# Prompt-attention masks moved from TensorE into VectorE's maximum, and the compression gather split into halves of eight tokens with two buffers

## The chip, the cores and the metric

The kernel runs on one NeuronCore of a Trainium2 chip as a single launch. The metric is the device time of one execution in microseconds (us). The core's engines run side by side: TensorE (PE; its weight loads are listed as PEld), VectorE (DVE), ScalarE (ACT), GpSimd (POOL) and SyncE (SP, which here only issues DMAs). Each works through its own instructions in a fixed order and waits for the others at semaphores.

## The reference, cut to what matters

One step of a decoder layer for two groups of requests: a prompt of 1024 tokens, and 8 samples with 8 new tokens each and 2048 cached ones. The layer is a half feed-forward, a mixer (attention beside a state-space branch), and a second half feed-forward. Attention has 8 query heads over 2 key/value heads of 64, and three branches: compressed blocks, selected blocks and a window of 512. With 16 blocks of 64 covering all 1024 prompt tokens, a prompt query's selected branch is plain causal attention. The parts that the change touches:

```
# masked softmax of each branch; the window branch adds dist < 512
def masked_softmax(s, mask):
    s = jnp.where(mask, s.astype(jnp.float32), NEG)
    e = jnp.where(mask, jnp.exp(s - jnp.max(s, axis=-1, keepdims=True)), 0.0)
    return e / jnp.maximum(jnp.sum(e, axis=-1, keepdims=True), 1e-30)
...
# compression of the cached rows: windows of 32 tokens, stride 16, through a two-layer MLP
    ch = rows[:, :nc * CMP_STRIDE].reshape(b, nc, CMP_STRIDE, KV_HEADS, HEAD_DIM)
    blk = jnp.concatenate([ch[:, :-1], ch[:, 1:]], axis=2) + pe[None, None, :, None, :]
    blk = blk.transpose(0, 1, 3, 2, 4).reshape(b, nc - 1, KV_HEADS, CMP_BLOCK * HEAD_DIM)
    return jax.nn.silu(blk @ w1) @ w2
```

## The kernel before, in words

The program is written in layer order, but the order of instructions on each engine is set at build time by a scheduler that follows data dependences, buffer reuse and modelled durations. Pools with a fixed number of buffers (`bufs`) say when a tile can be written again. A table `KN` picks the engine of each copy or scaling, and the order of the query tiles.

The stage concerned is the loop over eight tiles of 128 prompt queries (L1751), in the order 2, 7, 6, 5, 4, 3, 1, 0. Two things are written into this loop.

**Prompt attention.** For each tile there are two key/value groups of four heads, and two branches: branch 0 sees all keys up to the tile, branch 1 (window) the last five key tiles at most. Per head and branch the keys are cut into one part of up to 512 keys or two parts. Each part is one bank of PSUM, from three buffers (`s2`) that the compressed branch's scores share. Two fp32r matmuls (L1808, L1810) form the scores with the positional bias. The mask is added on TensorE: a bf16 matmul of the identity with a 128x128 mask of zeros and very large negative numbers adds it into the last 128 columns of the part (`mdiag`, causal) or the first 128 (`medge`, window edge), L1813. VectorE takes the negated maximum (L1818, or L1821 per part and L1822 over the two). ScalarE computes the exponential from PSUM into `pb` in SBUF and its sum (L1824). `pb` is scaled by the gate over the sum on POOL, ACT or DVE (L275 to L279), transposed on TensorE (L1846), copied out of PSUM to `pt` (L267), and multiplied with the values (L1855). `pb` has five buffers per branch.

**Compression of the samples.** `compress_sample` runs for the eight samples, at places that `KN["cs"]` gives: three before the first query tile, then 0, 2, 1, 1, 0, 1, 0. One indirect DMA on POOL's queue (L1689) gathers a sample's rows into `chk` (128 chunks of 16 tokens, 16 KB each, 2 MB in all), with a single buffer. Eight steps (keys, then values, four steps each) follow: ACT and POOL copy four tokens into `chp`, TensorE transposes them to `cT` (L1712), ACT casts the upper part `th`, DVE forms the remainder `tl` (L1717), and twelve matmuls accumulate into `cA` (L1733 to L1735). At the end of keys and of values follow a SiLU and a small product `c` (L1740, L1743). The copies of step `jj` read tokens 4jj to 4jj+3 of the buffer, once for keys and once for values.

**What comes next.** The sample attention uses the memory that this stage's pools give back when they close. Its first transfers therefore wait for the last matmul of compression, which reads the last tile of these pools: on SP's queue two window loads of `schk` (L2052), `big` (2.3 MB, L1951), four loads of `xT` and the loads of the output projection's weights `raw` (L1900); on POOL's queue the gathers of `schk` (L2048, 512 KB each). The output projection (`wout`, L250 to L252) and the sample attention's transposes (`kT_ps`, L2064) are the first work on TensorE after the stage.

Of the kernel before, what the change touches and what calls it, by code (L numbers as in the profile page):

```python
# [10 lines left out]
F32 = mybir.dt.float32  # L11
# [7 lines left out]
P = 128  # L19
# [22 lines left out]
def f32(ap):  # L42
    return ap.bitcast(F32)
# [37 lines left out]
def hybrid_step(ctx: ExitStack, tc: tile.TileContext, *aps):  # L81
# [1499 lines left out]
    AC = Ds.enter_context(pool("attc"))  # L1581
    mdiag = AC.tile([P, P], BF16, name="mdiag")
    medge = AC.tile([P, P], BF16, name="medge")
    mcmp = AC.tile([P, 8, 64], BF16, name="mcmp")
    for t_ in (mdiag, medge, mcmp):
        nc.gpsimd.memset(t_, 0.0)
# [9 lines left out]
                            base=-31, channel_multiplier=1)  # L1596

    QBs = [AC.tile([P, 4, P], F32R, name=f"QB{i}") for i in range(4)]
    ABs = ExitStack()
# [74 lines left out]
    with pool("att", bufs=2) as K, pool("att_ps2", bufs=3, space=PSUM) as PS2, \  # L1674
# [5 lines left out]

        ch_cmp = A["cache_cmp"][0].rearrange("n (c s) k g d -> (n c) (s k g d)", s=16)
        with tc.issue_after(wload.ins):
# [3 lines left out]

        def gather(b):
            chk = CK.tile([P, 16, 2, 2, 64], F32, name="chk", bufs=1)
            nc.gpsimd.indirect_dma_start(  # L1689
                out=chk.rearrange("p s k g d -> p (s k g d)"), out_offset=None, in_=ch_cmp,  # L1690
                in_offset=bass.IndirectOffsetOnAxis(ap=idx[:, b:b + 1], axis=0))
            return chk

        first_chk = gather(0)

# [5 lines left out]

        def compress_sample(b):
            chk = gather(b) if b else first_chk
            def pairs(kv, jj):
                chp = CK.tile([P, 2, 2, 2, 64], F32, name="chp", bufs=1)
                for g in range(2):
                    copy(KN["chp"][g], chp[:, :, g], chk[:, 4 * jj:4 * jj + 4, kv, g, :].rearrange(
                        "p (j r) d -> p j r d", r=2))
# [42 lines left out]
        for qi, qt in enumerate(KN["qt"]):  # L1751
# [33 lines left out]
            for g in range(2):  # L1785
                PT = {}
                for br in range(2):
# [6 lines left out]
                    for hh_ in range(4):  # L1794
# [3 lines left out]
                        for i in range(ns):  # L1798
                            pn = P * ((nk // P - st // P) // (ns - i))
                            s = PS2.tile([P, 512], F32, name="s2", tag="s2")[:, :pn]  # L1800
                            parts.append((s, st, pn))
                            kk = slice(P * k0 + st, P * k0 + st + pn)
                            masks = []
                            if st + pn == nk:
                                masks.append((pn - P, mdiag))
                            if br == 1 and qt >= 4 and st == 0:
                                masks.append((0, medge))
# [9 lines left out]
                        if ns == 1:  # L1817
                            nc.vector.tensor_reduce(mx[:, 0:1], parts[0][0], axis=AX.X, op=OP.max, negate=True)  # L1818
                        else:
                            for i in range(2):  # L1820
                                nc.vector.tensor_reduce(mx[:, 1 + i:2 + i], parts[i][0], axis=AX.X, op=OP.max)  # L1821
                            nc.vector.tensor_reduce(mx[:, 0:1], mx[:, 1:3], axis=AX.X, op=OP.max, negate=True)  # L1822
                        for i, (s, st, pn) in enumerate(parts):
                            nc.scalar.activation(pb[:, st:st + pn], s, AF.Exp, bias=mx[:, 0:1],  # L1824
                                                 accum_out=part[:, hh_, i:i + 1])
                    total = part[:, :, 0]
# [706 lines left out]
```

## Time and profile before

| what | value |
|---|---|
| median of three runs | 2472.01 us (2469.42 to 2479.5) |
| profiled execution, its time | 2475.45 us |
| its span (first to last instruction) | 2473.8 us, so 1.65 us lie outside |
| TensorE's mean granted clock | 0.987 of full speed |
| TensorE busy in the span | 2408.8 us (97%) |
| VectorE, ScalarE, GpSimd busy | 1744.7, 1131.2, 418.3 us (71%, 46%, 17%) |
| stage of prompt attention | about 1137 to 1548 us of the span |

How to read it: the busy shares are averages over the whole span, and the change touches one stage of about 410 us, so the tables below are cut to that stage. A matmul's listed duration is the time from its start to its modelled end, and neighbouring matmuls overlap; what a matmul costs TensorE is the distance from its start to the start of the next. "Idle before" in a group of instructions is time in which the engine waited, with the instruction that ended the wait.

### The profile page before, as it was taken

What the parts mean: (1) busy time and instruction counts of PE and PEld (TensorE: products, weight loads), DVE (VectorE), ACT (ScalarE), POOL (GpSimd) and SP (SyncE); (2) the same over time, 40 slices, a digit from 0 to 9 for tenths busy, and PEclk for the clock granted to TensorE, in tenths of its full rate; (3) what the DMA queues carried; (4) which work ended last, traced back from release to release, by engine and by line L of the source; (5) the groups of instructions that cost most, each with busy time, mean ns of one, the idle gap of its engine ahead of it and who ended that gap; (6) DMA issues with size and microseconds to landing.
All of it is one profiled execution on the core that took longest, in us unless ns stands there. A gap on an engine that the chain in (4) does not pass through costs nothing.

```text
span 2473.8 us, 48193 instructions
## 1 busy us (share of the span) xinstructions
PE 2408.8 (97%) x19026; PEld 2222.8 (90%) x19026; DVE 1744.7 (71%) x3673; ACT 1131.2 (46%) x2501; POOL 418.3 (17%) x533
## 2 busy tenths in 40 slices
PE   7999999999999999999999999999999999999998
PEld 6999999999999998997667766677899999999998
DVE  6777776677778855655656666777967676768776
ACT  7544444441133254425666675444545454543113
POOL 0000000011134343333434343111000000001110
PEclk9999999999999999999999998999999999999999
DMA  4334343598652333423110104476235353559654
GB/s 162 134 133 160 130 164 129 175 338 306 230 190 84 126 116 102 119 69 127 40 64 35 69 35 148 130 250 213 89 123 171 120 174 120 174 213 370 238 209 153
DMA packets 230446, 379.07 MB, mean 153 GB/s; under 512 B 18509, under 2 KB 147705, under 8 KB 228812
## 3 DMA queue, kind: packets, MB, share of 16 engines
q1 hardware_dynamic: 210248, 318.02, 37.7%
q0 software_dynamic: 7600, 38.59, 4.5%
q10 hardware_dynamic: 12372, 19.38, 2.2%
q8 instruction: 150, 2.46, 0.4%
q14 instruction: 76, 0.62, 0.1%
HBM read 255.66 MB, written 124.40 MB: 154 GB/s over the span
## 4 chain that ended last, share of the span: by engine, by line
PE 86%; DVE 6%; DMA 4%; ACT 3%; issue 1%; POOL 0%; ACTq 0%; DVEq 0%; POOLq 0%
PE dq L634 6%; PE gY L367 6%; PE dq L633 6%; PE dq L635 6%; PE gY L368 6%; PE gY L366 6%; PE gX L367 5%; PE gX L366 5%; PE gX L368 5%; PE o L1855 3%; PE pT L1846 3%; PE s L1808 1%; PE xbc L250 1%; PE xbc L251 1%; PE xbc L252 1%; PE cA L1733 1%
## 5 line engine op out<-in xcount | busy, mean ns | idle before, releaser
L634 PE MATMUL dq<-db,da 128*128 128x256 f32 (+1 forms) x1232 | 353.2, 288 | 0.3 <-DVE da L270 0.3
L635 PE MATMUL dq<-db,da 128*128 128x256 f32 (+1 forms) x1232 | 352.8, 288 | 0.0
L633 PE MATMUL dq<-db,da 128*128 128x256 f32 (+1 forms) x1232 | 349.8, 288 | 2.7 <-DVE Cc L386 2.2
L642 DVE TENSOR_TENSOR xT<-xT,dq 128x256 f32<-128x256 f32 (+1 forms) x456 | 186.9, 432 | 84.8 <-PE dq L635 83.2
L270 POOL TENSOR_TENSOR ds<-dw 128x512 f32<-128x512 f32 x22 | 29.5, 1341 | 1228.1 <-DVE wlo L270 508.0
L633 PEld LDWEIGHTS dq<-db,da 128*128 128x128 f32 x1232 | 230.5, 189 | 3.3 <-DVE Cc L386 2.5
L635 PEld LDWEIGHTS dq<-db,da 128*128 128x128 f32 x1232 | 232.8, 189 | 0.0
L634 PEld LDWEIGHTS dq<-db,da 128*128 128x128 f32 x1232 | 231.9, 188 | 0.6 <-DVE da L270 0.5
L267 ACT CAST whi<-ws 128x512 fp32r<-128x512 f32 x156 | 96.5, 623 | 205.9 <-PE gY L368 137.6
L270 DVE TENSOR_TENSOR wlo<-raw,whi 128x512 fp32r<-128x512 f32 x184 | 125.5, 687 | 83.9 <-ACT whi L267 83.5
L267 ACT CAST da<-ds 128x512 fp32r<-128x512 f32 x88 | 52.6, 623 | 234.7 <-PE dq L635 93.4
L267 ACT CAST whi<-raw 128x512 fp32r<-128x512 f32 x181 | 112.4, 626 | 72.0 <-PE g L414 19.5
L270 DVE TENSOR_TENSOR wlo<-ws,whi 128x512 fp32r<-128x512 f32 x156 | 106.7, 687 | 42.4 <-ACT whi L267 41.9
L1824 ACT ACTIVATE pb<-s,mx 128x256 f32<-128x256 f32 (+3 forms) x192 | 105.0, 552 | 59.7 <-DVE mx L1822 37.6
L1846 PEld LDWEIGHTS pT<-ident,pb 128*128 128x128 f32 x528 | 59.6, 143 | 45.8 <-issue 40.1
L1821 DVE TENSOR_REDUCE mx<-s 128x1 f32<-128x384 f32 (+2 forms) x128 | 66.6, 536 | 44.0 <-PE s L1813 34.1
L366 PE MATMUL gY<-B3h,whi 128*128 128x256 f32 (+1 forms) x320 | 91.5, 287 | 1.5 <-ACT whi L267 1.4
L366 PE MATMUL gX<-B6h,whi 128*128 128x256 f32 (+1 forms) x320 | 91.3, 286 | 0.9 <-ACT Cc L373 0.9
L367 PE MATMUL gX<-B6h,wlo 128*128 128x256 f32 (+1 forms) x320 | 91.4, 286 | 0.6 <-DVE wlo L270 0.6
L367 PE MATMUL gY<-B3h,wlo 128*128 128x256 f32 (+1 forms) x320 | 91.6, 287 | 0.2 <-DVE wlo L270 0.2
L277 POOL TENSOR_TENSOR pb<-pb,sm 128x640 f32<-128x640 f32 (+7 forms) x70 | 85.1, 1238 | 37.6 <-DVE sm L1831 34.0
L367 PE MATMUL gY<-B2h,wlo 128*128 128x256 f32 (+1 forms) x320 | 91.4, 286 | 0.0
(763 smaller groups left out, 8548.1 us busy)
## 6 DMA issues: line engine op xcount, KB each, us to landing
db<-GD SPq DMA_DIRECT2D x42, 1632.0 KB
GD<-Cc SPq DMA_DIRECT2D x154, 272.0 KB
GD<-his SPq DMA_DIRECT2D x84, 272.0 KB
raw<-in_ffn_wu_dram SPq DMA_DIRECT2D x22, 1024.0 KB
dw<-in_ffn_wd_dram SPq DMA_DIRECT2D x44, 512.0 KB
raw<-in_ffn_wg_dram SPq DMA_DIRECT2D x21, 1024.0 KB
GD<-hp SPq DMA_DIRECT2D x70, 272.0 KB
db<-GD SPq DMA_DIRECT2D x14, 1088.0 KB
```

The costliest lines, as they stand in the source:

```text
L267: return nc.scalar.copy(out, src) if eng == "a" else ENGINES[eng].tensor_copy(out, src)
L270: ENGINES[eng].tensor_tensor(out, x, y, op=op)
L277: nc.gpsimd.tensor_tensor(out, x, by.to_broadcast(list(x.shape)), op=OP.mult)
L366: nc.tensor.matmul(q, ah[:, k], b_, start=first, stop=False, skip_group_check=True)
L367: nc.tensor.matmul(q, al[:, k], b_, start=False, stop=False, skip_group_check=True)
L368: nc.tensor.matmul(q, ah[:, k], c_, start=False, stop=(k == 3), skip_group_check=True)
L633: nc.tensor.matmul(q, x, bh[:, u, o], start=first, stop=False, skip_group_check=True)
L634: nc.tensor.matmul(q, y, bh[:, u, o], start=False, stop=False, skip_group_check=True)
L635: nc.tensor.matmul(q, x, bl[:, u, o], start=False, stop=(u == np_ - 1), skip_group_check=True)
L642: nc.vector.tensor_tensor(x, x, q, op=OP.subtract if i == 4 else OP.add)
L1824: nc.scalar.activation(pb[:, st:st + pn], s, AF.Exp, bias=mx[:, 0:1], accum_out=part[:, hh_, i:i + 1])
L1846: nc.tensor.transpose(tq_[:kn, P * hh_:P * hh_ + P], src, ident)
```

## The change

The two mask tiles become the ends of one row `mrow` of 5 x 128 columns, with zeros between: the row's last pn columns are the causal mask of a part of pn keys, its first pn columns the window's edge mask. The 160 mask matmuls and their weight loads go. In the 160 masked parts (of 192) the maximum's instruction becomes `tensor_tensor_reduce`: it adds scores and mask, multiplies by -1, writes the result into the part's slice of `pb`, and reduces it with a minimum, which is the negated maximum. The exponential of these parts reads `pb` (SBUF) in place and scales by -1. Parts without a mask keep the plain reduction, now negated per part, and the reduction over two parts is a minimum.

The gather is cut in two: `idx2` (two small VectorE instructions, once) holds the index of each 8-token half, `chk` has half the size and two buffers, and half `u` of the next sample is gathered right behind the last step that copies out of half `u`. There are 16 gathers of 1 MB in place of 8 of 2 MB. Nothing else in the source changes; later lines move down by three to five.

```
-    mdiag = AC.tile([P, P], BF16, name="mdiag")
-    medge = AC.tile([P, P], BF16, name="medge")
+    mrow = AC.tile([P, 5 * P], BF16, name="mrow")
+    medge, mdiag = mrow[:, :P], mrow[:, 4 * P:]
...
+    idx2 = AC.tile([P, 2, 8], I32, name="idx2")
+    for u in range(2):
+        nc.vector.tensor_scalar(idx2[:, u], idx, 2.0, float(u), op0=OP.mult, op1=OP.add)
...
-        def gather(b):
-            chk = CK.tile([P, 16, 2, 2, 64], F32, name="chk", bufs=1)
+        def gather(b, u):
+            chk = CK.tile([P, 8, 2, 2, 64], F32, name="chk", bufs=2)
...
-                in_offset=bass.IndirectOffsetOnAxis(ap=idx[:, b:b + 1], axis=0))
+                in_offset=bass.IndirectOffsetOnAxis(ap=idx2[:, u, b:b + 1], axis=0))
...
-        first_chk = gather(0)
+        chks = [gather(0, u) for u in range(2)]
...
         def compress_sample(b):
-            chk = gather(b) if b else first_chk
             def pairs(kv, jj):
+                chk = chks[jj // 2]
...
                 nc.vector.tensor_tensor(tl[:, :, :256], sv, f32(th[:, :, :256]), op=OP.subtract)
+                if kv and jj % 2 and b < 7:
+                    chks[jj // 2] = gather(b + 1, jj // 2)
...
-                            nc.tensor.matmul(s, QBq[g][:97, hh_], KB[:97, br, g, kk], start=False, stop=not masks,
+                            nc.tensor.matmul(s, QBq[g][:97, hh_], KB[:97, br, g, kk], start=False, stop=True,
                                              skip_group_check=True)
-                            for j, (c, mk) in enumerate(masks):
-                                nc.tensor.matmul(s[:, c:c + P], identb, mk, start=False,
-                                                 stop=(j == len(masks) - 1), skip_group_check=True)
...
+                            if mask is None:
+                                nc.vector.tensor_reduce(m_, s, axis=AX.X, op=OP.max, negate=True)
+                            else:
+                                nc.vector.tensor_tensor_reduce(out=p_, in0=s, in1=mask, scale=-1.0, scalar=3e38,
+                                                               op0=OP.add, op1=OP.min, accum_out=m_)
+                        if ns == 2:
+                            nc.vector.tensor_reduce(mx[:, 0:1], mx[:, 1:3], axis=AX.X, op=OP.min)
+                        for i, (s, mask, p_) in enumerate(parts):
+                            nc.scalar.activation(p_, s if mask is None else p_, AF.Exp, bias=mx[:, 0:1],
+                                                 scale=1.0 if mask is None else -1.0, accum_out=part[:, hh_, i:i + 1])
```

The scheduler builds a new order from this. The first scores of the stage on TensorE, before (`s` with a number is a buffer of scores; `identb` the bf16 identity):

```order
L1808 MATMUL s_14377<-KA,QA 128x384
L1810 MATMUL s_14377<-KB,QB_13182 128x384
L1813 LDWEIGHTS identb
L1813 MATMUL s_14377<-mdiag,identb 128x128
L1808 MATMUL s_14385<-KA,QA 128x384
L1810 MATMUL s_14385<-KB,QB_13182 128x384
L1813 LDWEIGHTS identb
L1813 MATMUL s_14385<-mdiag,identb 128x128
```

And after the change:

```order
L1812 MATMUL s_14388<-KA,QA 128x384
L1814 MATMUL s_14388<-KB,QB_13183 128x384
L1812 MATMUL s_14395<-KA,QA 128x384
L1814 MATMUL s_14395<-KB,QB_13183 128x384
L1812 MATMUL s_14402<-KA,QA 128x384
L1814 MATMUL s_14402<-KB,QB_13183 128x384
```

Every masked part has lost a weight load and a matmul; here the pairs of score matmuls follow each other directly.

The end of the stage on TensorE, before: the last group of value products `o` and what follows it (the last compression matmul `cA` stands 149 rows ahead of the first row shown).

```order
L1846 MATMUL pT<-ident,pc 64x128 x4
L1855 MATMUL o<-pt,VA 64x512 x2
L1855 MATMUL o<-pt,VAc 64x512
L1985 MATMUL a_ps<-gates,big 128x24
L2064 MATMUL kT_ps<-ident,schk 128x128 x8
L2096 LDWEIGHTS zrow
L2096 MATMUL so<-oneh,zrow 128x384
```

After the change, the same last value products and the rows behind them:

```order
L1851 MATMUL pT<-ident,pc 64x128 x4
L1860 MATMUL o<-pt,VA 64x512 x2
L1715 MATMUL cT<-ident,chp 128x128 x4
L1860 MATMUL o<-pt,VAc 64x512
L1738 MATMUL cA<-th_13756,w1h 128x256
L1739 MATMUL cA<-th_13756,w1l 128x256
L1715 MATMUL cT<-ident,chp 128x128 x4
L1740 MATMUL cA<-tl_13757,w1h 128x256
```

The last of these compression matmuls, some 100 rows further down, and what follows:

```order
L1738 MATMUL cA<-th_13760,w1h 128x256
L1739 MATMUL cA<-th_13760,w1l 128x256
L1740 MATMUL cA<-tl_13761,w1h 128x256
L1748 MATMUL c_17986<-w_179,cxh 127x64 x2
L2101 LDWEIGHTS zrow
L2101 MATMUL so<-oneh,zrow 128x384
L2069 MATMUL kT_ps<-ident,schk 128x128 x8
L2076 MATMUL s_ps<-skT,QS 64x512 x2
L250 MATMUL wout<-oh,whi 128x512 x2
```

All eight steps of the eighth sample, which stood ahead of the last value products, now stand behind them.

POOL's queue at the same place, before (`schk` are the sample attention's gathers):

```order
L267 COPY chp<-chk 128x2x128 x3
L277 TENSOR_TENSOR pb_18160<-pb_18160,sm 128x256
L270 TENSOR_TENSOR pc<-pc,sm 128x512
L267 CAST QA<-QA 64x2x128
L270 TENSOR_TENSOR QB_13184<-qT,QA 64x2x128
L277 TENSOR_TENSOR pb_18199<-pb_18199,sm 128x256
L2048 DMA schk<-in_cache_sel_dram,idx_9814 128x1024
L277 TENSOR_TENSOR pb_18284<-pb_18284,sm 128x256
L2048 DMA schk<-in_cache_sel_dram,idx_9814 128x1024 x3
```

And after the change:

```order
L1692 DMA chk<-in_cache_cmp_dram,idx_13180 128x2048
L277 TENSOR_TENSOR pb_18324<-pb_18324,sm 128x128
L267 COPY chp<-chk 128x2x128 x2
L270 TENSOR_TENSOR pc<-pc,sm 128x512
L1692 DMA chk<-in_cache_cmp_dram,idx_13180 128x2048
L267 COPY chp<-chk 128x2x128
L277 TENSOR_TENSOR pb_18424<-pb_18424,sm 128x128
L267 COPY chp<-chk 128x2x128
L1968 MEMSET QS 128x512
L1979 MEMSET zrow 32x128
L267 COPY chp<-chk 128x2x128 x6
L2053 DMA schk<-in_cache_sel_dram,idx_9814 128x1024 x32
```

The eighth sample's two gathers now stand among the scalings of the last query tile, and all 32 `schk` gathers behind the last compression copy.

## Rows read from the trace of the kernel before

**Rows 1.** Busy time by engine, granted clock, DMA share, GB/s, in three stretches.

```profile
1137.00:1531.00 394.00, 382.78 (x2594) 277.22 (x2594) 255.14 (x599) 258.10 (x689) 153.40 (x227) 1.00 0.16 61
1531.00:1556.00 25.00, 22.72 (x90) 12.68 (x89) 16.06 (x61) 14.30 (x43) 5.91 (x8) 0.62 0.56 187
1515.00:1530.00 15.00, 14.41 (x100) 9.70 (x100) 12.49 (x37) 9.47 (x32) 6.74 (x9) 1.00 0.93 366
```

**Rows 2.** Mask weight loads, 1130 to 1545 us: count; busy, mean ns; idle before.

```profile
L1813 PEld LDWEIGHTS <-identb 128*128 128x128 bf16 x160 | 15.8, 99 | 21.2 <-issue 19.0
```

**Rows 3.** Timeline of PE around two masks: start, us, instruction.

```profile
1194.94 0.23 PE L1813 MATMUL s<-medge,identb 128*128 128x128 bf16 x1
1195.01 0.39 PE L1846 MATMUL pT<-ident,pb 128*128 128x128 f32 x2
...
1217.70 0.23 PE L1813 MATMUL s<-medge,identb 128*128 128x128 bf16 x1
1217.74 0.36 PE L1733 MATMUL cA<-th,w1h 128*128 128x256 f32 x1
1217.94 0.28 PE L1734 MATMUL cA<-th,w1l 128*128 128x256 f32 x1
1218.06 0.38 PE L1712 MATMUL cT<-ident,chp 128*128 128x128 f32 x2
```

**Rows 4.** Groups of the stage: the maximum over 512 columns.

```profile
L1821 DVE TENSOR_REDUCE mx<-s 128x1 f32<-128x512 f32 x24 | 16.2, 686 | 11.1 <-PE s L1813 8.0 <-PE s L1810 3.0
```

**Rows 5.** Line 2080: its instructions (min/median/max ns), then one on VectorE's timeline.

```profile
L2080 DVE CUSTOM_DVE_ANT_0 S<-s_ps,big x20: 660/688/692, 1555.8 to 1721.1; 128x512 f32<-128x512 f32 x20
...
1556.39 0.08 DVE L2080 DVE_READ_ACCUMULATOR2_ANT smxs<- 128x1 f32 x1
1556.39 0.28 DVE L2004 TENSOR_SCALAR pcg<-spc,grow 128x127 f32<-128x127 f32 x1
```

**Rows 6.** Groups of the stage: ScalarE over 512 columns, from PSUM, SBUF, SBUF.

```profile
L1824 ACT ACTIVATE pb<-s,mx 128x512 f32<-128x512 f32 x40 | 27.2, 685 | 6.9 <-DVE mx L1822 3.6 <-DVE mx L1818 2.4 <-PE pT L1846 1.0
...
L275 ACT ACTIVATE pb<-pb,sm 128x512 f32<-128x512 f32 x4 | 2.9, 725 | 0.0
...
L1777 ACT ACTIVATE pc<-pc 128x512 f32<-128x512 f32 x8 | 5.0, 631 | 1.8 <-DVE pc L1776 1.8
```

**Rows 7.** Waits of the stage: who for whom, us, times, longest.

```profile
POOL chp L267 <- DMA chk<-in_cache_cmp_dram,idx: 16.1, 7, 8.7
...
PEld s L1808 <- ACT pb L1824: 8.5, 15, 0.9
...
ACT chp L267 <- DMA chk<-in_cache_cmp_dram,idx: 7.9, 5, 3.1
...
PEld cA L1733 <- ACT pb L1824: 4.1, 5, 0.8
```

**Rows 8.** Groups of the stage: issue of the compression gather.

```profile
L1689 POOL DMA_INDIRECT chk<-in_cache_cmp_dram,idx x8 | 8.2, 1022 | 11.7 <-DVE qT L1621 7.1 <-ACT chp L267 3.4 <-POOL chp L267 0.5
```

**Rows 9.** Tile `chk`: its transfers, from issue to landing.

```profile
DMA to landing us min/median/max: 8.3/9.5/14.8
```

**Rows 10.** Timelines of PE and SP: last compression matmul, and SP's first issues.

```profile
1514.59 0.28 PE L1735 MATMUL cA<-tl,w1h 128*128 128x256 f32 x1
...
1514.90 0.83 SPq L2052 DMA_DIRECT2D schk<-in_cache_win_dram  x2
```

**Rows 11.** Groups of the stage: the two steps between `cT` and `cA`.

```profile
L1717 DVE TENSOR_TENSOR tl<-cT,th 128x512 fp32r<-128x512 f32 x64 | 44.0, 687 | 16.6 <-ACT th L267 16.1
...
L267 ACT CAST th<-cT 128x512 fp32r<-128x512 f32 x64 | 37.5, 586 | 26.2 <-PE cT L1712 25.8
```

**Rows 12.** Tile `schk`: its transfers, from issue to landing.

```profile
DMA to landing us min/median/max: 4.2/6.0/12.3
```

**Rows 13.** Timelines of SP and PE at the stage's end.

```profile
1544.80 12.87 SPq L1900 DMA_DIRECT2D raw<-in_w_out_dram  x6
...
1546.57 1.39 PE L1855 MATMUL o<-pt,VAc 64*64 64x512 f32 x2
1549.88 0.63 PE L2064 MATMUL kT_ps<-ident,schk 128*128 128x128 f32 x4 [1.00 <-DMA raw<-in_w_out_dram]
...
1555.47 1.20 PE L250 MATMUL wout<-oh,whi 128*128 128x512 f32 x2
```

More of the change, by code (lines that the diff above doesn't have):

```diff
@@ L1581, in hybrid_step @@
     AC = Ds.enter_context(pool("attc"))
-    mdiag = AC.tile([P, P], BF16, name="mdiag")
-    medge = AC.tile([P, P], BF16, name="medge")
+    mrow = AC.tile([P, 5 * P], BF16, name="mrow")
+    medge, mdiag = mrow[:, :P], mrow[:, 4 * P:]
     mcmp = AC.tile([P, 8, 64], BF16, name="mcmp")
-    for t_ in (mdiag, medge, mcmp):
+    for t_ in (mrow, mcmp):
         nc.gpsimd.memset(t_, 0.0)
@@ L1678, in b1 @@
             return PS1.tile([P, 512], F32, name=name, tag=tag, bufs=2 if name == "pT" else 1)
-        ch_cmp = A["cache_cmp"][0].rearrange("n (c s) k g d -> (n c) (s k g d)", s=16)
+        ch_cmp = A["cache_cmp"][0].rearrange("n (c s) k g d -> (n c) (s k g d)", s=8)
         with tc.issue_after(wload.ins):
@@ L1702, in compress_sample @@
         def compress_sample(b):
-            chk = gather(b) if b else first_chk
             def pairs(kv, jj):
+                chk = chks[jj // 2]
                 chp = CK.tile([P, 2, 2, 2, 64], F32, name="chp", bufs=1)
                 for g in range(2):
-                    copy(KN["chp"][g], chp[:, :, g], chk[:, 4 * jj:4 * jj + 4, kv, g, :].rearrange(
+                    copy(KN["chp"][g], chp[:, :, g], chk[:, 4 * (jj % 2):4 * (jj % 2) + 4, kv, g, :].rearrange(
                         "p (j r) d -> p j r d", r=2))
@@ L1800, in hybrid_step @@
                             s = PS2.tile([P, 512], F32, name="s2", tag="s2")[:, :pn]
-                            parts.append((s, st, pn))
                             kk = slice(P * k0 + st, P * k0 + st + pn)
-                            masks = []
+                            mask = None
                             if st + pn == nk:
-                                masks.append((pn - P, mdiag))
-                            if br == 1 and qt >= 4 and st == 0:
-                                masks.append((0, medge))
+                                mask = mrow[:, 5 * P - pn:]
+                            elif br == 1 and qt >= 4 and st == 0:
+                                mask = mrow[:, :pn]
@@ L1808, in hybrid_step @@
                             nc.tensor.matmul(s, QAs[g][:, hh_], KA[:, br, g, kk], start=True, stop=False,
                                              skip_group_check=True)
-                            nc.tensor.matmul(s, QBq[g][:97, hh_], KB[:97, br, g, kk], start=False, stop=not masks,
+                            nc.tensor.matmul(s, QBq[g][:97, hh_], KB[:97, br, g, kk], start=False, stop=True,
                                              skip_group_check=True)
-                            for j, (c, mk) in enumerate(masks):
-                                nc.tensor.matmul(s[:, c:c + P], identb, mk, start=False,
-                                                 stop=(j == len(masks) - 1), skip_group_check=True)
+                            parts.append((s, mask, pb[:, st:st + pn]))
@@ L1815, in hybrid_step @@
                             st += pn
                         mx = K.tile([P, 3], F32, name="mx", bufs=4)
[L1817 to L1822, printed above, removed]
@@ L1823, in hybrid_step @@
-                        for i, (s, st, pn) in enumerate(parts):
-                            nc.scalar.activation(pb[:, st:st + pn], s, AF.Exp, bias=mx[:, 0:1],
-                                                 accum_out=part[:, hh_, i:i + 1])
+                        for i, (s, mask, p_) in enumerate(parts):
+                            m_ = mx[:, 1 + i:2 + i] if ns == 2 else mx[:, 0:1]
+                            if mask is None:
[3 more added lines that the diff above has]
+                                                               op0=OP.add, op1=OP.min, accum_out=m_)
@@ L1826, in hybrid_step @@
+                        if ns == 2:
+                            nc.vector.tensor_reduce(mx[:, 0:1], mx[:, 1:3], axis=AX.X, op=OP.min)
+                        for i, (s, mask, p_) in enumerate(parts):
+                            nc.scalar.activation(p_, s if mask is None else p_, AF.Exp, bias=mx[:, 0:1],
+                                                 scale=1.0 if mask is None else -1.0, accum_out=part[:, hh_, i:i + 1])
                     total = part[:, :, 0]
```

## The prediction

> **What bounds the kernel now.** I first read the busy time by stretch, because the change lies in one stage of a long program [rows 1]. [...] From 1531 to 1556 us the picture changes: TensorE is listed as busy 22.72 of 25 us, but at a mean clock of 0.62. Its work there is 22.72 x 0.62 = 14 us at full clock; this end loses 11 us already now. Ahead of it, from 1515 to 1530 us, the transfers run at a share of 0.93 and 366 GB/s, some 15 x 0.366 = 5.5 MB, while TensorE is busy 14.41 of 15 us: the loads of the next stage are covered by the last query tiles.
>
> Then TensorE's timeline, for starts and not durations [rows 3], the waits of the stage [rows 7], and the groups of the instructions that are replaced [rows 4 to 6].
>
> **The masks leave TensorE.** 160 mask matmuls go [rows 2]. The listed 0.23 us each is not their cost, since neighbours overlap. Behind a mask a 256-column cA matmul starts after 0.04 us, but the matmul after that one only 0.20 us later (1217.74 to 1217.94), where 0.12 is normal (1217.94 to 1218.06). So this mask costs 0.04 + 0.08 = 0.12 us [rows 3]. Ahead of a transpose it costs 0.07 (1194.94 to 1195.01). In the order of before 87 masks are followed by an fp32r matmul and 73 by transposes or value products, which I price alike: 87 x 0.12 + 73 x 0.07 = **15.5 us less**. If every mask cost 0.07, it is 11.2 us; at 0.12 throughout, 19.2. The work is on the path wherever TensorE does not wait; its waits in this stretch are some 11 of 394 us, so nearly all counts.
>
> [...]
>
> **The maximum with a mask on VectorE.** The plain maximum over 512 columns takes 0.686 us [rows 4]. The instruction that replaces it is already in the kernel at line 2080: same operation from PSUM and SBUF to SBUF over 512 columns, median 688 ns, and behind it a read of the accumulator of 83 ns; on the timeline the next instruction starts together with that read (both at 1556.39) [rows 5]. So VectorE gains nothing to do, or at most 160 x 0.083 = 13.3 us of its 255. The mask in bf16 is not shown by any row; the bound below is the plain maximum (0), the bound above the read in full. Beside a VectorE at 65% I take +1 us on TensorE, for parts where a score's chain ends last, out of 0 to +3.
>
> **The exponential reads SBUF.** From PSUM 512 columns take 685 ns; two other ScalarE operations from SBUF take 725 and 631 [rows 6]. So 160 of them cost ScalarE between -8.6 and +6.4 us of its 258; cover is TensorE's 383 us. I take 0. If the cover is gone the upper bound lies within the +3 above. [...]
>
> **PSUM comes free earlier.** A masked part's scores are read for the last time by VectorE and no longer by the exponential behind it. TensorE waits for the exponential 8.5 us ahead of scores and 4.1 us ahead of cA, which stands behind them in the queue [rows 7]. The gain is 0 to 12.6 us. Since the next wait is for VectorE, the engine just ahead, I take a third: **-4 us**. Against it, VectorE now writes `pb`, and waits in its order until the transposes of the earlier contents are done; the five buffers cover this, as they cover ScalarE's writes now.
>
> **The gather in halves.** ACT's and POOL's copies wait 7.9 and 16.1 us for the rows [rows 7], TensorE hardly. A transfer lands 9.5 us after its issue in the median [rows 9]; with two buffers it starts about half a sample earlier. POOL pays 8 more issues of 1.02 us [rows 8], hidden on an engine that is busy 39%. What stands behind an issue that waits for its buffer is the next `chp` copy or a `pb` scaling; both have slack. I take **-1 us** of TensorE, out of -3 to +2.
>
> **What the new order does to the end.** This is the term against the change. Before, the last compression matmul starts at 1514.59 us and the sample attention's loads follow at once, SP's first at 1514.90 [rows 10]; from there they run beside the attention's tail. In the new order all eight steps of the eighth sample stand behind the last value products, and the loads still wait for the last compression matmul: SP's window rows, `raw`, `big`, `xT`, and POOL's 32 gathers behind the last `chp` copies. Their cover is gone. Three parts:
> - The attention's tail loses its half clock, as compression's matmuls come between its waits: the 11 us lost now can come back whole.
> - The lone steps: `th` and `tl` take 0.586 and 0.687 us [rows 11], 1.27 us in series, against 12 x 0.12 = 1.44 us of cA matmuls of the step before. They nearly hide; 1.5 us for eight steps.
> - Behind the last matmul TensorE waits. `schk` lands 6.0 us after issue in the median, 12.3 at most [rows 12]; `raw`, issued at 1544.80, was waited for until 1549.88, 5.1 us later [rows 13]; the whole 5.5 MB need 15 us at 366 GB/s. Little work is there from about 6 us and a steady flow at 15; I take 12 us lost, and 4 more for the clock, half of a stretch like the one now between the last value products at 1546.57 and the first `wout` at 1555.47 (8.9 us) [rows 13].
>
> After loses 12 + 4 + 1.5 = 17.5, before 11: **+6.5 us**. Bounds: fed after 6.0 us with the clock kept, 6 - 11 = -5; 15 us with half clock over as long a stretch again, 15 + 1.5 + 12 - 11 = +17.5.
>
> **The sum:** -15.5 + 1 - 4 - 1 + 6.5 = -13 us. The profiled execution took 2475.45 us (1.65 outside its span), 3.4 above the median of the runs, so 2462.4 as profiled, and **2459 us** against the median of 2472.01.
>
> **Rivals.**
> - *The lost cover eats the gain.* With the end at +16 and no gain from PSUM: -15.5 + 1 - 1 + 16 = 0.5, so about 2472. For it: the 15 us of transfers at a 0.93 share that stand under the attention now. Against: the projection can start on its first two `raw` tiles.
> - *A larger gain.* The waits for the exponential vanish whole (-12.6) and the end costs nothing: -15.5 + 1 - 12.6 - 1 = -28, 2444 us. For it: ScalarE holds the buffer a further 0.685 us per part. Against: three buffers at TensorE's pace are waited for by something.
> - *Slower: the next stage waits for all its loads.* Behind the last compression matmul 5.5 MB and POOL's first eight gathers (4 MB) share the queues: 9.5 / 0.366 = 26 us. If TensorE gets nothing steady until then, and half clock for the next 13 us, the end loses 26 + 1.5 + 13 = 40, +29 against before: -15.5 + 29 + 1 = +14.5, 2486 us. It decides from an end that costs 27 us more than now. Against: queues run side by side, and median landings are 6 us.
> - *The masks cost only their own slot.* Some 9 us instead of 15.5: 2465 us. Against: the 0.20 us in the rows.
> - *The change doesn't do what it says:* the masked maximum runs at half rate, 160 x up to 0.686 = 110 us more, VectorE near 365 of 394 and as tight as TensorE; some 2475 to 2490 us. Against: line 2080's 688 ns.
>
> **How the numbers follow.** Forecast 0.50; lost cover 0.22; larger gain 0.16; slower by the loads 0.07; smaller masks 0.03; half rate 0.02. Half a per cent, about what a measurement of this kernel can tell from no change, is 12.4 us: faster is below 2459.6, slower above 2484.4. The forecast lies on that line; I count 0.28 of its 0.50 as faster, with the larger gain 0.44. Same: 0.22 + 0.22 + 0.03 = 0.47. Slower: 0.09. The forecast's own range from its bounds is 2450 to 2466; the range for 8 in 10 takes in most of both neighbours, 2444 to 2478.
>
> **What would show it.** The masked maximum at 0.69 us over 512 columns, with the next instruction beside the accumulator's read. No 0.20 us between cA matmuls behind scores. TensorE's wait for `pb` ahead of scores below 8.5 us. The last cA matmul after the last value products, SP's first `schk` right behind it, and a stretch of half clock and waits for `schk` or `raw` of 10 to 20 us there, where the attention's tail runs at full clock. Wrong would be: TensorE's stretch up to the last value products not shorter, compression not behind attention, or an end that stands still for over 25 us.

## The result, and the profile after

The changed kernel takes 2489.74 us (median of 7 runs, 2486.63 to 2501.79) against 2472.01 us. The ratio is 1.0081, with a 95% interval from 1.0066 to 1.0095: slower by some 20 us, where 13 us less were forecast. The profiled execution took 2489.03 us, with a span of 2487.3 (before 2475.45 and 2473.8); its span is 13.5 us longer.

I cut the span at two points: the end of the stage (the last `cA` or `o`, whichever is later) and the last `wout`. First the three tiles before, then after (min/median/max ns, first to last start):

```profile
L1735 PE MATMUL cA<-tl,w1h x256: 277/282/562, 1157.1 to 1514.6; 128*128 128x256 f32 x128
L1855 PE MATMUL o<-pt,VAc x32: 589/640/1109, 1162.3 to 1547.4; 64*64 64x512 f32 x32
L252 PE MATMUL wout<-ol,whi x192: 288/296/628, 1556.9 to 1753.3; 128*128 128x288 f32 x128, 128*128 128x512 f32 x64
```

```profile
L1740 PE MATMUL cA<-tl,w1h x256: 277/282/561, 1153.0 to 1533.3; 128*128 128x256 f32 x128
L1860 PE MATMUL o<-pt,VAc x32: 589/614/641, 1170.5 to 1511.0; 64*64 64x512 f32 x32
L252 PE MATMUL wout<-ol,whi x192: 288/297/628, 1552.2 to 1767.2; 128*128 128x288 f32 x128, 128*128 128x512 f32 x64
```

Before, attention ends last, 32.8 us behind compression; after, compression ends last, 22.3 us behind attention. From the first scores (1138.2 before, 1138.6 after) to that end it takes 409.2 us before and 394.7 after: 14.5 less. From there to the last `wout` it is 205.9 and 233.9: 28.0 more. The difference is +13.5, that of the spans. The 14.5 us are close to the 13 us forecast for the whole kernel, but only by chance: the prediction's terms for the stage alone add up to some 25 us less, and those for the next stage to some 12.5 us more ("Why the prediction was wrong" works this out).

The replaced instructions on VectorE took as long as was forecast. These are groups of the stage after:

```profile
L1824 DVE CUSTOM_DVE_ANT_0 pb<-s,mrow 128x512 f32<-128x512 f32 x32 | 21.4, 686 | 6.1 <-PE s L1814 4.0 <-PE pT L1851 2.0
L1824 DVE DVE_READ_ACCUMULATOR2_ANT mx<- 128x1 f32 x160 | 13.2, 82 | 0.0
L1829 ACT ACTIVATE pb<-pb,mx 128x512 f32<-128x512 f32 x32 | 22.9, 715 | 3.4 <-DVE mx L1824 3.3
L1715 PE MATMUL cT<-ident,chp 128*128 128x128 f32 x256 | 42.4, 282 | 11.1 <-ACT pb L1829 3.1 <-ACT pb L275 2.5 <-DVE tl L1720 1.8
```

686 ns with a mask, 686 without [rows 4]; the exponential from SBUF takes 715 ns against 685 [rows 6]. The waits after (who for whom: us, times, longest):

```profile
DVE pb L1824 <- PE pT L1851: 8.1, 6, 3.7
...
PEld s L1812 <- DVE mx L1824: 3.7, 8, 1.0
...
PEld s L1812 <- DVE mx L1827: 1.6, 2, 0.8
...
POOL chp L267 <- DMA chk<-in_cache_cmp_dram,idx: 2.4, 1, 2.4
...
ACT whi L267 <- DMA raw<-in_w_out_dram: 9.4, 2, 5.9
```

TensorE's 8.5 us for the exponential ahead of scores became 3.7 us for VectorE's maximum and 1.6 for its reduction over two parts, and POOL's 16.1 us for gathered rows became 2.4 [rows 7]. New is the first line: VectorE, which now writes `pb`, waits until its earlier contents are transposed. The seam between the stages after, on SP's queue and on TensorE:

```profile
1533.66 0.83 SPq L2057 DMA_DIRECT2D schk<-in_cache_win_dram  x2
...
1535.88 0.94 SPq L1905 DMA_DIRECT2D raw<-in_w_out_dram  x2
...
1537.17 0.34 SPq L1956 DMA_DIRECT2D big<-saD  x1
...
1537.56 16.49 SPq L1897 DMA_DIRECT2D xT<-xD  x4
```

```profile
1537.51 0.98 PE L2069 MATMUL kT_ps<-ident,schk 128*128 128x128 f32 x4 [1.44 <-DMA schk<-in_cache_win_dram]
...
1540.51 1.98 PE L2076 MATMUL s_ps<-skT,QS 128*64 128x512 f32 x4 [0.68 <-ACT skT L267]
...
1547.00 0.79 PE L250 MATMUL wout<-oh,whi 128*128 128x512 f32 x1 [4.51 <-ACT whi L267]
...
1551.18 0.80 PE L250 MATMUL wout<-oh,whi 128*128 128x512 f32 x1 [3.39 <-ACT whi L267]
```

The first load leaves 0.4 us behind the start of the stage's last matmul; before it left 32.5 us ahead of it (1514.90, [rows 10]). The first `wout` waits for weights until 1547.00 and the second until 1551.18. The same loss by stretches (PE busy is the first number behind the length, the granted clock stands ahead of the DMA share), after, then before:

```profile
1533.00:1547.00 14.00, 5.58 (x24) 2.65 (x22) 0.74 (x3) 2.67 (x5) 6.57 (x7) 0.67 0.91 337
1547.00:1560.00 13.00, 9.05 (x34) 6.41 (x34) 3.19 (x11) 1.09 (x2) 0.00 (x0) 0.70 1.05 404
1560.00:1600.00 40.00, 35.08 (x237) 24.85 (x237) 26.92 (x64) 16.03 (x36) 1.92 (x2) 0.87 0.36 112
1600.00:1650.00 50.00, 50.00 (x428) 35.28 (x429) 38.38 (x98) 23.76 (x50) 6.79 (x7) 1.00 0.64 206
1650.00:1700.00 50.00, 46.59 (x477) 37.12 (x480) 36.36 (x95) 18.91 (x38) 10.90 (x10) 0.97 0.70 225
1700.00:1767.00 67.00, 60.77 (x628) 49.89 (x617) 54.49 (x165) 36.10 (x89) 5.75 (x6) 0.90 0.63 196
```

```profile
1547.00:1555.00 8.00, 6.64 (x27) 2.83 (x26) 6.09 (x18) 6.04 (x14) 0.00 (x0) 0.71 0.42 135
1555.00:1568.00 13.00, 13.00 (x73) 9.95 (x72) 9.49 (x26) 4.23 (x8) 0.00 (x0) 0.90 0.33 100
1568.00:1600.00 32.00, 32.00 (x250) 22.73 (x249) 24.29 (x53) 13.25 (x27) 2.49 (x3) 1.00 0.40 123
1600.00:1650.00 50.00, 49.27 (x473) 35.45 (x471) 38.05 (x108) 25.48 (x51) 10.31 (x11) 1.00 0.76 237
1650.00:1700.00 50.00, 47.56 (x510) 37.03 (x509) 39.50 (x104) 21.27 (x45) 11.70 (x12) 1.00 0.74 241
1700.00:1753.00 53.00, 48.21 (x477) 40.43 (x478) 42.60 (x132) 29.69 (x76) 0.17 (x1) 0.94 0.60 189
```

I take busy time times granted clock for the work at full clock. Added up, it is 190.4 us after and 190.5 before: the same work. Time lost to waits and to the lower clock is the rest: 234 - 190.4 = 43.6 us after, 206 - 190.5 = 15.5 before, so 28.1 more. This is an estimate, since busy share and clock are means of long stretches; over windows of 10 us it is 41.5 and 15.5. Of after's loss 16.9 us lie in the first 27 us (before 4.6 in the first 21), 9.5 in the next 40, and 17.1 from 1600 on (before 10.9).

### The profile page after: what moved, and what is told of

It reads as the page before. It is cut to its first block, busy times and chain, and to the rows that moved or that the text cites. A ratio compares the mean times of both kernels' runs of the same rounds, so it can differ in the third digit from the quotient of the medians.

```text
span 2487.3 us, 48028 instructions
## 1 busy us (share of the span) xinstructions
PE 2399.2 (96%) x18866; PEld 2225.3 (89%) x18866; DVE 1753.4 (70%) x3835; ACT 1135.1 (46%) x2501; POOL 425.8 (17%) x540
## 4 chain that ended last, share of the span: by engine, by line
PE 86%; DVE 7%; DMA 4%; ACT 2%; issue 1%; SPq 0%; ACTq 0%; DVEq 0%; POOLq 0%
PE gY L367 6%; PE gY L366 6%; PE gY L368 6%; PE dq L633 6%; PE dq L634 6%; PE dq L635 6%; PE gX L367 5%; PE gX L366 5%; PE gX L368 5%; PE o L1860 3%; PE pT L1851 3%; PE xbc L250 1%; PE xbc L251 1%; PE xbc L252 1%; PE cA L1740 1%; PE s L1812 1%
## 5 line engine op out<-in xcount | busy, mean ns | idle before, releaser
L1829 ACT ACTIVATE pb<-pb,mx 128x384 f32<-128x384 f32 (+3 forms) x160 | 92.1, 577 | 28.5 <-DVE mx L1824 18.1
L1824 DVE CUSTOM_DVE_ANT_0 pb<-s,mrow 128x384 f32<-128x384 f32 (+3 forms) x160 | 78.3, 512 | 26.2 <-PE s L1814 16.7
L366 PE MATMUL gX<-B7h,whi 128*128 128x256 f32 (+1 forms) x320 | 91.3, 285 | 0.4 <-ACT Cc L377 0.4
```

Source lines behind the costliest of these rows:

```text
L366: nc.tensor.matmul(q, ah[:, k], b_, start=first, stop=False, skip_group_check=True)
L1829: nc.scalar.activation(p_, s if mask is None else p_, AF.Exp, bias=mx[:, 0:1], scale=1.0 if mask is None else -1.0, accum_out=part[:, hh_, ...
```

## The experiments

My theory was that the place of compression's last sample costs the time, because the next stage's loads then start without lead; the rivals were the gathers and the masked maximum itself (below, A is my theory, B and C are the rivals). All ratios are to the kernel before, timed beside each run (its medians there were 2470.73 to 2473.84 us), with 95% intervals. "Stage", "next" and "lead" are read as above from one profile each (lead: end of the stage minus SP's first `schk`).

| run | median us | ratio | stage | lead | next |
|---|---|---|---|---|---|
| before | 2472.01 | 1 | 409.2 | 32.5 | 205.9 |
| after | 2489.74 | 1.0081 (1.0066 to 1.0095) | 394.7 | -0.4 | 233.9 |
| e1_masks | 2493.75 | 1.0086 (1.0069 to 1.0103) | 401.2 | -0.3 | 228.9 |
| e2_gathers | 2476.86 | 1.0022 (1.0009 to 1.0035) | 412.7 | 32.4 | 208.1 |
| e3_ordered | 2492.43 | 1.0077 (1.0058 to 1.0096) | 418.8 | 49.8 | 208.5 |
| e4_loads_late | 2494.77 | 1.0099 (1.0075 to 1.0124) | 404.2 | -1.0 | 224.4 |
| e5_in_place | 2472.85 | 1.0010 (0.9997 to 1.0024) | 405.7 | 26.6 | 206.8 |
| e6_in_place_masks | 2485.38 | 1.0062 (1.0043 to 1.0080) | 407.3 | 19.6 | 214.5 |
| e7_no_masks | 2472.55 | 1.0011 (0.9998 to 1.0024) | 404.4 | 34.5 | 206.5 |
| e8_both | 2497.18 | 1.0111 (1.0094 to 1.0128) | 401.6 | -0.4 | 232.8 |
| e9_no_masks_old_order | 2467.85 | 0.9980 (0.9970 to 0.9990) | 398.4 | 30.7 | 207.7 |
| e10_in_place_old_order | 2475.43 | 1.0002 (0.9989 to 1.0015) | 400.0 | 29.9 | 210.5 |
| e11_halves_in_place_old_order | 2473.39 | 0.9996 (0.9983 to 1.0009) | 402.6 | 31.0 | 204.7 |
| e12_gathers_old_order | 2472.86 | 0.9998 (0.9986 to 1.0011) | 406.2 | 28.9 | 206.3 |
| e13_late_compression | 2512.85 | 1.0164 (1.0141 to 1.0186) | 416.9 | -0.3 | 232.0 |
| e14_lead_one_tile | 2477.69 | 1.0021 (1.0008 to 1.0035) | 409.4 | 22.4 | 212.2 |
| e15_lead_paced | 2473.66 | 0.9999 (0.9985 to 1.0014) | 402.9 | 19.9 | 204.8 |

The profiled execution of a run lies up to 9 us off its median (e14: 2486.92 against 2477.69; e7: 2481.59 against 2472.55; e4: 2489.61 against 2494.77). The first scores start at 1137.6 to 1143.4 us, but at 1147.9 in e7, so its stage is not comparable. Differences of a few us between rows of the last three columns say nothing.

**The halves of the change.** e1 is the diff's mask part alone, e2 its gather part alone.

> The mask half of the change alone: masks added by VectorE, gathers as before (8 of 2 MB, one buffer). In its order 11 of the 64 compression steps stand behind the last value products (8 with the whole change, none before). Theory A (the loss is the order at the end: compression ends behind attention, so the next stage's loads start without cover, about +28 us against -14.6 us saved up to the last compression matmul): as slow as the whole change or slower, 2485 to 2500 us, SP's first schk load behind the last value product. Theory B (the 16 smaller gathers are what costs): the saving alone, about 2457 us. Theory C (the masked maximum on VectorE costs more than the masks did, in the stage itself): 2485 to 2495 us too, but with a stage that ends no earlier than before (1547.9 us).

> The gather half alone: 16 gathers of 1 MB with two buffers, masks on TensorE as before. In its order compression ends ahead of the last three groups of value products, as before. A: 2465 to 2475 us, POOL's and ACT's waits for chk (16.1 and 7.9 us before) mostly gone, loads of the next stage still under the attention's tail. B: 2482 us or more. C: about 2472 us.

The masks alone carry the whole loss, with compression 11 steps behind attention, where after has 8. The gathers alone cost 0.2%, some 2 us more than A allowed.

**Compression ahead again (e3).** The changed kernel, with the scores of five query tiles queued behind the last `cA` of a sample:

```diff
+        last_cA, behind_cA = {}, {2: 1, 3: 3, 4: 4, 5: 6, 6: 7}   # tile's place: sample
-                            nc.tensor.matmul(ab, wh, ml, ...)
+                            last_cA[b] = nc.tensor.matmul(ab, wh, ml, ...)
+                if qi in behind_cA and h == 0:   # sc: the tile's first score matmul
+                    tc.add_manual_dep(sc.ins, last_cA[behind_cA[qi]].ins.name, NoSync)
```

In `KN["cs"]` the eighth sample is written one place earlier.

> The whole change, but TensorE's first scores of the query tiles at places 2, 3, 4, 5 and 6 of the loop are queued behind the last compression matmul of samples 1, 3, 4, 6 and 7 (issue order only); compression then ends ahead of the last five groups of value products. Nothing is left out. A: the cover is back and the masks' saving stays: 2452 to 2466 us, the first wout products within some 10 us of the last value product. B and C: 2484 to 2495 us, as the whole change, since gathers and maximum are unchanged.

The next stage came back (208.5), yet the time did not. Compression now ended 50 us ahead of attention, and attention alone could not fill TensorE: in the last 50 us its work at full clock is 43.85 x 0.73 = 32 us. That is not all of it, as the stretch up to compression's end lost some 25 us too (12 in before). A's forecast was missed. The end of the stage in e3, and VectorE's wait:

```profile
1512.00:1562.00 50.00, 43.85 (x193) 25.45 (x191) 35.65 (x144) 28.12 (x92) 14.30 (x20) 0.73 0.56 203
```

```profile
DVE pb L1829 <- PE pT L1856: 13.3, 9, 3.7
```

So early compression is no cure by itself: compression's matmuls are what TensorE does between attention's waits.

**The loads held back (e4).** The kernel before, with the next stage's first loads made to wait for the last value product:

```diff
+    def behind_o(dma):
+        tc.add_manual_dep(dma.ins, last_o.ins.name, Sync)
-        nc.sync.dma_start(big, saD)
+        behind_o(nc.sync.dma_start(big, saD))    # as are xT (z == 0) and schk of the first pair
```

> The kernel before, with the same order of computation, but the next stage's first loads (big, the first two window loads and gathers of schk, the four xT loads) wait for the last value product of attention. Only the cover of these transfers is taken away. A: 15 to 25 us slower than before, 2487 to 2497 us, with TensorE waiting for schk, raw and big at half clock behind about 1548 us. B and C: within 5 us of before, since neither gathers nor maximum are touched.

The missing lead alone costs 18.5 us in the next stage and 0.99% of the time. (The stage itself is 5 us shorter in this profile; whether the loads under it had cost that is not shown, as e12, with its loads there, is 3 us shorter too.) TensorE in e4:

```profile
1541.38 1.07 PE L1855 MATMUL o<-pt,VAc 64*64 64x512 f32 x2
...
1551.89 0.62 PE L1992 MATMUL a_ps<-gates,big 64*128 64x24 f32 x2 [9.18 <-DMA big<-saD]
1554.45 1.12 PE L2073 MATMUL kT_ps<-ident,schk 128*128 128x128 f32 x4 [0.97 <-DMA schk<-in_cache_win_dram]
...
1566.66 0.80 PE L250 MATMUL wout<-oh,whi 128*128 128x512 f32 x1 [5.84 <-ACT whi L267]
```

**The masked maximum written in place (e5, e6).** The negated masked scores go back into their PSUM bank; e6 has the gathers of before.

```diff
-    nc.vector.tensor_tensor_reduce(out=p_, in0=s, ...)
+    nc.vector.tensor_tensor_reduce(out=s, in0=s, ...)
-    nc.scalar.activation(p_, s if mask is None else p_, AF.Exp, ...)
+    nc.scalar.activation(p_, s, AF.Exp, ...)
```

> The whole change, but the masked maximum writes scores plus mask back in place into PSUM, and the exponential reads PSUM as before; pb is written by ScalarE alone again. Nothing is left out. In its order compression ends ahead of the last four groups of value products, as before the change. Theory D (VectorE's write into pb needs the buffer a step earlier and waits in VectorE's order for the transposes of its old contents; compression falls back, ends behind attention, and the next loads lose their cover): 2452 to 2466 us, VectorE's waits for pT transposes at the maximum gone (8.1 us with the change, 14.7 in the ordered run). Theory C (the masked maximum itself or the lost filler costs it): 2485 us or more.

> As the in-place kernel, but with the gathers of before (8 of 2 MB, one buffer). D: 2450 to 2466 us, and the difference to the in-place kernel is what the gather halves cost or bring with compression in its old place; by the run with the gathers alone they cost about 5 us. Theory C: 2485 us or more.

In e5 the scheduler puts compression early again (all 64 steps ahead of the 13th of the 16 groups of value products, as in before; after has 56 ahead of the last), and the loss is gone, though the saving that D forecast did not come. VectorE hardly waits for transposes:

```profile
DVE s L1824 <- PE pT L1851: 1.0, 1, 1.0
```

e6 has 0.6% of loss left (lead 19.6, next 214.5), outside the range of D. What remains is not explained by the lead, since e15 has the same lead and no loss; e10 shows that it goes with the order.

**Masks left out, or paid twice (e7, e8).** e7 is the kernel before without `masks.append(...)`, so no mask is applied. e8 is e1 with the mask matmul kept beside the masked maximum.

> The kernel before without the masks of the selected and window branches: the 160 mask matmuls are left out, maximum, exponential and gathers are as before (so the result leaves out these masks). Its order keeps compression ahead of the last five groups of value products. It gives the price of the mask matmuls alone: by the rows before 15.5 us, 2454 to 2460 us. By theory C's rival form (attention's tail is bound by its chain and not by TensorE, so masks cost little): 2466 to 2474 us.

> Masks stay on TensorE and VectorE's masked maximum into pb is there as well (the masks count twice, which changes no softmax weight); gathers as before. Its order has 8 compression steps behind the last value products, as with the change. D: the maximum's write into pb moves the order, not the missing mask matmuls: loss without the saving, 2500 to 2512 us. If the missing matmuls are what moved it: 2470 to 2478 us.

Without masks and with the scheduler's own order there is no gain (e7). With masks on both engines the order is the late one (e8). So the late place comes with VectorE's write into `pb` (e1, e8 and after have it, e5 and e6 do not), not with the missing matmuls (e7). Why the scheduler does so is open. e8 beside e1 says more: with the 160 mask matmuls back on TensorE its stage is 401.6 us, against 401.2 without them.

**The order of before kept (e9 to e12).** A table sets the neighbours on TensorE, VectorE, ScalarE and POOL as in before (the half gathers' DMAs are free):

```diff
+    for eng, steps in OLD_ORDER.items():
+        for a_, b_ in zip(order, order[1:]):
+            tc.add_manual_dep(mine[b_], mine[a_].name, NoSync)
```

e9: no masks applied. e10: e6. e11: e5. e12: e2.

> The masks of the selected and window branches left out (result without them), maximum, exponential and gathers as before, and in this stage the order of before on TensorE, VectorE, ScalarE and GpSimd, instruction by instruction, with only the 160 mask matmuls missing. It asks whether TensorE's time for the masks was on the path. Theory P (TensorE's issue bounds the stage, and the run without masks gained nothing only because it was given another order): 2472 - 15.5, 2453 to 2461 us. Theory Q (the stage follows chains through VectorE and ScalarE whose waits fill what TensorE gives up): 2467 to 2475 us.

> Masks added by VectorE in place in PSUM, gathers as before, the order of before in this stage instruction by instruction (the masked maximum where the maximum was, no mask matmuls). Nothing is left out. P: 2453 to 2463 us, far from the 2485 us that the same kernel took in its own order. Q: 2467 to 2478 us. If the accumulator's read or the mask's second operand cost VectorE what it has not: above the run without masks by 5 us or more.

> As the in-place kernel in the order of before, with the gathers in halves and two buffers as in the change (the gathers themselves are not held to a place in POOL's order). Nothing is left out. P: as the run with the gathers of before or up to 3 us faster, 2450 to 2463 us. If the 16 gathers cost something by themselves, as the run with the gather half alone hints (+5 us): 3 to 8 us slower than with the gathers of before.

> The kernel before with the gathers in halves and two buffers, all other instructions of the stage in the order of before. Nothing is left out. If the +5 us of the gather half alone came from its other order: 2465 to 2473 us. If the 16 gathers cost it: 2474 to 2480 us.

This prices the parts. Masks leaving TensorE give 4.9 us (e9, 0.9980). The masked maximum in place takes that back (e10, 1.0002). These two fall in theory Q's ranges and outside P's. Halved gathers give nothing (e12; e11 beside e10), so e2's 0.2% came with its order. TensorE in e9, scores followed by compression:

```profile
1220.60 0.28 PE L1811 MATMUL s<-KB,QB 97*128 97x256 f32 x1
1220.72 0.28 PE L1737 MATMUL cA<-th,w1h 128*128 128x256 f32 x1
1220.84 0.28 PE L1738 MATMUL cA<-th,w1l 128*128 128x256 f32 x1
1220.96 0.60 PE L1716 MATMUL cT<-ident,chp 128*128 128x128 f32 x4
1221.32 0.36 PE L1739 MATMUL cA<-tl,w1h 128*128 128x256 f32 x1
1221.52 0.28 PE L1737 MATMUL cA<-th,w1h 128*128 128x256 f32 x1
```

It is 0.12 us from matmul to matmul behind the scores: the 0.20 us of [rows 3] went with the mask. Behind the four transposes the same 0.20 us stays (1221.32 to 1221.52).

**Late compression in before (e13).** The eighth sample is queued behind the last value product:

```diff
+        compress_sample(next(sequences), mm)   # its first transposes NoSync behind mm, the last o
```

> The kernel before (masks on TensorE, gathers whole), with one thing moved: the eighth sample's compression is queued behind the last value product of attention, as it comes to stand with the change. Nothing is left out. If the late place alone makes the loss: 2488 to 2502 us, first schk load behind the last value product, some 222 to 234 us from the end of compression to the last wout (206 before). If VectorE's write into pb is needed for the loss: within 8 us of before.

```profile
L1738 PE MATMUL cA<-tl,w1h x256: 277/282/563, 1158.5 to 1555.3; 128*128 128x256 f32 x128
...
L1858 PE MATMUL o<-pt,VAc x32: 589/614/641, 1163.7 to 1531.0; 64*64 64x512 f32 x32
...
L252 PE MATMUL wout<-ol,whi x192: 288/297/628, 1573.4 to 1787.3; 128*128 128x288 f32 x128, 128*128 128x512 f32 x64
```

With every mask still on TensorE, the place of eight steps alone costs 1.64%: the stage ends 24 us behind attention (1531.0 to 1555.3) and is 7.7 us longer, and the next stage takes 26.1 us more. The loss is above the range of 2488 to 2502 us; the next stage lies in its own range. Here the first 56 steps stand as in before, so that the last six groups of value products have no compression between them; in after the steps are spread up to the last group.

**The changed kernel, paced (e14, e15).** As e3, but `behind_cA` is `{6: 6, 7: 7}` in e14 (the last two tiles) and `{3: 3, 4: 4, 5: 5, 6: 6, 7: 7}` in e15.

> The whole change, with TensorE's first scores of the last but one query tile queued behind the last compression matmul of the seventh sample, those of the last tile behind the eighth's. Compression ends ahead of the last group of value products but one. If the lost cover is the main cost: the loads get some 10 to 20 us of lead, stage plus next stage 10 us shorter than with the change, 2474 to 2484 us. If VectorE's waits for pb cost as much by themselves: 2486 to 2495 us, as the run with the stronger ordering (2492).

> The whole change, with first scores of the query tiles at places 3, 4, 5, 6 and 7 queued behind the last compression matmul of samples 3, 4, 5, 6 and 7: compression is paced over the tiles and ends one tile ahead of attention. Lost cover as main cost: 2472 to 2484 us. Waits for pb by themselves: 2486 to 2495 us.

```profile
L1742 PE MATMUL cA<-tl,w1h x256: 277/282/562, 1155.8 to 1523.7; 128*128 128x256 f32 x128
...
L1865 PE MATMUL o<-pt,VAc x32: 589/614/680, 1174.2 to 1543.9; 64*64 64x512 f32 x32
...
L252 PE MATMUL wout<-ol,whi x192: 291/296/503, 1553.9 to 1748.7; 128*128 128x288 f32 x128, 128*128 128x512 f32 x64
```

The whole change, with one query tile left behind compression, is at 0.9999 when compression is paced over the tiles (e15): the 0.8% are gone, and no gain is left. With the last two samples alone held in place (e14) 0.2% of loss remains. Both medians lie in the range of the lost cover, below that of the waits for `pb`. No version beat before with its result kept.

## Why the prediction was wrong

- **Masks (-15.5).** As work, right: busy time times granted clock over the stage, added over windows of about 10 us, is 389.1 us before, 374.6 in e9 (-14.5) and 370.9 after (-18.2); kernels with the same work differ by up to some 7 us in this measure. As time, too large: e9 gained 4.9 us. Its stage is 10.8 us shorter in its profile, since lost time rose from 20.1 to 23.8 us, and the next stage is 1.8 longer; the rest, some 4 us, lies ahead of the stage and behind the last `wout`, where the source was not changed, and may be the spread of single profiles. That "nearly all counts" on a TensorE listed 97% busy (382.78 of 394 us, [rows 1]) was wrong, and e8 beside e1 agrees. The masks' own slots alone, 87 x 0.04 + 73 x 0.07 us [rows 3], are 8.6 us, an estimate. By work the trace of e9 shows more (14.5, with the weight loads and the delays behind the masks in it); the timed gain is smaller than either.
- **Masked maximum (+1, bound +3).** Its duration was right (686 ns), the accumulator's read (83 ns in the median) lies beside other work (after has one at 1403.69 us, with the next maximum started at 1403.69 too), and still it took back some 5 us (e10 against e9). Beside a VectorE busy 255.14 of 394 us [rows 1] the sum had only 1 us for it. That the cost comes from its place in the chain from scores to exponential is a guess that no run tests.
- **Exponential (0).** 30 ns more at 512 columns (715 against 685); no run prices this alone.
- **PSUM free earlier (-4).** Not seen as a gain: the wait ahead of scores for the reader of the bank fell from 8.5 to 5.3 us, but VectorE waits 8.1 us for the transposes of `pb`'s earlier contents. That "the five buffers cover this" was wrong.
- **Gathers (-1).** POOL's wait fell as forecast (16.1 to 2.4 us), TensorE gained nothing (e12, 0.9998).
- **The end (+6.5, bound +17.5): the step that failed.** The mechanism was named, and all of its signs came: last `cA` behind the last `o`, SP's `schk` right behind it, a lowered clock (0.67 and 0.70 from 1533 to 1560 us, where half was forecast), waits for `raw` (9.4 us on ScalarE). Even the 16 us behind the last `cA` were right for the first stretch (16.9 in 27 us). Three things were not.
  - The loss was ended with the first `wout` at full pace, but the rows go on: 9.5 us to 1600, 17.1 beyond, where before loses 10.9 from 1568 on. The next stage took 28.0 us more, where the terms give some 12.5: the 16, less the 3.5 of before's 11 us that lie behind its last `o`.
  - The 11 us that before loses were booked as recovered, yet lost time over the stage went from 20.1 to 23.8: 4.9 in the lone compression (22.3 us, where 1.5 was forecast as its extra), 18.9 ahead of it. So the stage gave 14.5 us of the 25.5 that its terms add up to (-15.5 + 1 - 4 - 1, then -7.5 for the part of the 11 us in the stage, and +1.5).
  - Behind its bound stood 15 us of transfers. With that bound the sum is still -2 us, or 2470, above the 2466 that the prediction calls the end of its own range; the measured time lies beyond both, so the bound was too small. The 5.1 us for `raw` [rows 13] were misread too: the profile puts that wait to `raw` at a transposition of `schk`, which does not read it. The first cast of `raw`, before and then after:

```profile
1551.92 1.15 ACT L267 CAST whi<-raw 128x512 fp32r<-128x512 f32 x2
```

```profile
1546.33 0.62 ACT L267 CAST whi<-raw 128x512 fp32r<-128x512 f32 x1 [5.87 <-DMA raw<-in_w_out_dram]
```

Before, the cast starts 7.1 us after the issue (1544.80) and waits for no load; after, it waits and starts 10.5 us after the issue (1535.88), with `big`, `xT` and the `schk` gathers issued around it. That these transfers delay `raw` is likely, but no run separates them.

The rival "the next stage waits for all its loads", at 0.07, came nearest: 2486 us, with +29 at the end. Its number is in part luck: it has TensorE get nothing steady for 26 us, while some 10 us of work at full clock were done in the first 27 and the loss was spread up to the last `wout`. Of its reasons against, queues did run side by side (before, 1515 to 1530 us: the two queues of SP's and POOL's transfers took 61.6% and 31.5% of the DMA engines' time); the median landing of 6 us was read from a stage whose loads had 32 us of lead, and over the whole stage it held again after (6.6 us). e4 and e13 show the mechanism without any other part of the change, e15 its removal. Why e13 and after lose some 8 us more in the next stage than e4 is open: there `raw` and the later gathers start late too, and the scheduler orders that stage otherwise.

## What to carry to other kernels

When a change makes a scheduler move work past the last reader of a buffer pool, price the whole next stage by the lead that its loads lose, not the gap up to its first matmul: here leads of some 20 us and more gave 205 to 215 us, and no lead 224 to 234. Filler work is worth most spread among the waits of a chain: too early (e3, 1.0077) cost as much as too late (after, 1.0081), and paced (e15, 0.9999) it cost nothing. And a TensorE listed as 97% busy need not hand back what is taken off it: here 14.5 us of work gave 4.9 us of time.

## What was not expected of the hardware

The 128-column bf16 mask matmul among fp32r matmuls cost more than its slot, 0.04 us ahead of `cA`: the second fp32r matmul behind it starts after 0.20 us where 0.12 is normal [rows 3], and e9 has 0.12 there in the rows shown. It is not a matter of bf16 alone: behind the fp32 transposes of e9 the first 256-column matmul is likewise followed only after 0.20 us, where among themselves these matmuls take 0.12. What the two have in common is not shown. The maximum that also adds a mask and writes 512 columns takes the same 686 ns as the plain one.
